# Linear-attention constants in a pool of their own made one stage earlier, and a fifth pair of the down projection by seven products

## The chip, the cores and the metric

One Trainium2 chip, of which the program uses one core. The metric is the device time of one execution in microseconds (us). The engines are TensorE (PE in the profile; its weight loads are PEld), VectorE (DVE), ScalarE (ACT), GpSimd (POOL) and SyncE (SP, which here issues transfers only).

## The reference

A trunk of four layers on a float32 input of 256 rows and 1024 columns. Each layer is a token mixer and a feed-forward part, and both end in a residual and a layer norm:

```python
for i in range(DEPTH):                      # DEPTH = 4
    kind = i % 3                            # 0 band attention, 1 gated linear attention, 2 differential attention
    y = mixer[kind](h)
    h = layer_norm(DN_ALPHA * h + y, ln1_g[i], ln1_b[i])
    g, u = split(h @ w_gate_up[i])          # 1024 -> 2 * 2816
    h = layer_norm(DN_ALPHA * h + (silu(g) * u) @ w_down[i], ln2_g[i], ln2_b[i])
```

The gated linear attention (the second layer's mixer) computes, beside its queries, keys, values and output gate, `log_a = log_sigmoid((x @ w_g1) @ w_g2 + b_g) / 16`, cumulative sums of it in chunks of 64 rows, a state for each chunk, and an rms norm with a gain `g_norm`.

## The kernel before

**Arithmetic.** Each float32 product is made of three TensorE products of rounded operands: every operand is split into a high part and a rest (`wh`, `wl` of the weights; two halves of `xT`, `plain`, `seven` of the data), and high by high, rest by high and high by rest are summed in PSUM. For every weight tile that arrives, ScalarE therefore casts the high part (L132, L145) and VectorE subtracts it for the rest (L133, L146) before TensorE can use it.

**Buffers.** Raw weights land in a ring of 24 KB per partition, split weights lie in a ring of 64 KB, in the order in which they are asked for; a split tile waits until the products that read the older tile at its place are done. Longer-lived tiles lie in the pool `act` (the residual `h`, the transposed input `xT`, small statistics with 16 buffers of each tag, `k1`). Everything else lies in a pool of the stage (`in_stage`: one mixer or one feed-forward part), opened when the stage begins and closed at its end; the next stage's pool takes the same place, and a tile there waits for the older tiles that it overlaps.

**Order.** The program is written out in full, without loops on the chip. `run_rows` and `run_cols` go through the weight tiles of a product; a clock of steps (`tick`) starts deferred pieces (`defer`): transposes of a finished norm, gate products, splits. A scheduler turns this into a fixed order of instructions for each engine, in which work that is ready may go ahead of earlier work that is not; on the chip each engine keeps that order.

**The mixer of layer 2** (`gla`, L656). It begins with its constants: a tile `cst` with a triangle of ones, the gain `g_norm` and two indicator columns; `g1t` with the split `w_g1` (memset L686, cast L687, subtraction L688); and `g2` with `w_g2` twice and `b_g` (memset L695, transfers L696 to L698). Then `gate1` (L716) is deferred by 2 steps, `gate2` (L736) by 3 more, `gate3` (L749) by 8 more, among the products of keys and output gate.

**The feed-forward part** (`ffn`). The 2816 hidden columns are 11 pairs of 128-column blocks. The up projection makes the pairs in order. A pair that is in `SEVEN = (0, 2, 4, 6)` is kept as four 128x128 blocks for each block product; GpSimd makes four sums and differences of them (`combine`), and ScalarE and VectorE split the seven results (`split`). The others are put into `plain`. The down projection goes through the pairs 0 to 7, loading pair c+1 before the products of pair c, and then the tail, pairs 8 to 10, first all rows of the first half (`t` = 0), then of the second:

- an ordinary pair takes 8 products of three matmuls each (`step`), and two casts and two subtractions of 128x1024 elements for its weights;
- a pair in `SEVEN` takes 7 products of three matmuls (`seven_products`), and for its weights three sums and differences on VectorE (L1017: one of 128x1024, two of 128x512 elements) and the casts and subtractions of seven blocks (one of 128x512, two of 128x1536 elements).

With the last pair of `SEVEN`, `gather` adds the sums that only these pairs use to `h`: nine VectorE additions of 128x512 elements, each after a product of that pair.

```python
for c in range(n_pairs - 3):
    load(c + 1)
    if c in SEVEN:
        seven_products(c)
        continue
    ...
for c in tail[1:]:
    load(c)
```

Of the kernel before, what the change touches and what calls it, by code (L numbers as in the profile page):

```python
# [9 lines left out]
F32 = mybir.dt.float32  # L10
F32R = mybir.dt.float32r
# [4 lines left out]
P = 128  # L16
# [17 lines left out]

SEVEN = (0, 2, 4, 6)


@with_exitstack  # L40
def trunk_kernel(
# [33 lines left out]
    act = ctx.enter_context(tc.tile_pool(name="act", bufs=1))  # L75
# [4 lines left out]
    def nm(s):  # L80
        uid[0] += 1
        return f"{s}_{uid[0]}"
# [5 lines left out]
    def in_stage(fn, *args, **kw):  # L88
        with tc.tile_pool(name=nm("stage"), bufs=1, reuse_waits="tile") as pool:
            stage.append(pool)  # L90
            fn(*args, **kw)
            stage.pop()

    def st(shape, dtype, tag, bufs):
        return stage[-1].tile(shape, dtype, tag=tag, bufs=bufs, name=nm(tag))

    def slab(shape, dtype=F32):
        return st(shape, dtype, "slab", 3)
# [4 lines left out]
    def k2(shape, dtype=F32):  # L103
        return st(shape, dtype, "k2", 12)
# [1 line left out]
    def k1(shape, dtype=F32):  # L106
        return act.tile(shape, dtype, tag="k1", bufs=5, name=nm("k1"))

    def small(shape, tag="small", bufs=16):
        return act.tile(shape, F32, tag=tag, bufs=bufs, name=nm(tag))  # L110

    def bank(tag="tp"):
# [5 lines left out]
    pad = const.tile([P, 32], F32, tag="powt", name="powt")  # L118
# [154 lines left out]
    def input_operand():  # L273

        return act.tile([P, NKT, 4 * P], F32R, tag="xT", bufs=1, name=nm("xT"))
# [377 lines left out]
        out_proj(OT, w_o, norm)  # L653


    def gla(xT, norm):  # L656
        HK, HV, NH = 128, 256, 4
        w_in = b_w_in
        w_g1, w_g2, b_g, g_norm = b_w_g1[0], b_w_g2[0], b_b_g[0], b_g_norm[0]
        cst = k2([P, 512])  # L660
        upper, gn, ind = cst[:, 0:P], cst[:, P : P + HV], cst[:, P + HV : P + HV + 2]
        nc.gpsimd.memset(cst, 0.0)
        for a in range(2):
# [17 lines left out]

        g1 = k1([P, NKT, 16])
        nc.gpsimd.dma_start(g1, w_g1.rearrange("(k p) n -> p k n", p=P))
        g1t = k2([P, 512], F32R)
        g1s = g1t[:, : 48 * NKT].rearrange("p (k n) -> p k n", n=48)
        nc.gpsimd.memset(g1t.bitcast(F32), 0.0)  # L686
        nc.scalar.copy(out=g1s[:, :, 0:16], in_=g1)  # L687
# [3 lines left out]
            in1=g1s[:, :, 0:16].bitcast(F32),  # L691
            op=ALU.subtract,
        )
        g2 = k2([P, 512])
        nc.gpsimd.memset(g2, 0.0)  # L695
        nc.gpsimd.dma_start(g2[0:16, :], w_g2)  # L696
        nc.gpsimd.dma_start(g2[32:48, :], w_g2)
        nc.gpsimd.dma_start(g2[64:65, :], b_g.unsqueeze(0))  # L698

        vo = slab([P, 2, 2, D])  # L700
        v, O = vo[:, 0, :, :], vo[:, 1, :, :]
# [190 lines left out]
    def ffn(xT, layer, norm):  # L892
# [8 lines left out]
        n_pairs = FFN // 256  # L901
        rest = [c for c in range(n_pairs) if c not in SEVEN]
        plain = st([P, 2 * len(rest), 4 * P], F32R, "plain", 1)

        def place_of(c):
            return 2 * rest.index(c)
# [17 lines left out]
        def split(c, f):  # L924
            x = seven[c] = st([P, 2, 7, P], F32R, "seven", len(SEVEN))
            nc.scalar.copy(out=x[:, 0], in_=f[:, 0:7, :])
            nc.vector.tensor_tensor(
                out=x[:, 1], in0=f[:, 0:7, :], in1=x[:, 0].bitcast(F32), op=ALU.subtract
            )
# [11 lines left out]
        def turn_hidden(c, t, hd):  # L941
            b = bank()
            for k in range(2):
                ks = slice(k * P, (k + 1) * P)
                nc.tensor.transpose(b[:, ks], hd[:, ks], ident)
            if c not in SEVEN:
                put(
# [17 lines left out]
        def col_done(c):  # L965
            g = {}

            def done(blk, b):
# [8 lines left out]
                gg = g.pop(k)  # L977
                if c not in SEVEN:
                    nc.vector.tensor_tensor(out=lo, in0=lo, in1=gg, op=ALU.mult)
# [15 lines left out]
        for c in range(2, FFN // 256):  # L995
            run_cols(w[c], src, col_done(c))
            if c >= 7:
                k = place_of(c)
                norm.load(
                    plain[:, k, 0:1].bitcast(F32), lambda sh: st(sh, F32, "gb", 4)  # L1000
                )
# [4 lines left out]
        def load(c):  # L1006
            raw = raw_ring.tile([P, 4, 512], F32, name=nm("raw"))
            nc.sync.dma_start(raw, w_down[layer, c].rearrange("p (k n) -> p k n", k=4))
            if c not in SEVEN:
                parts[c] = halves(raw[:, 0:2], 2) + halves(raw[:, 2:4], 2)  # L1010
# [39 lines left out]
        def seven_products(c):  # L1050
            for i, (a, b) in FORMS.items():
# [4 lines left out]
                    parts[c][b],  # L1056
                    c == SEVEN[-1] and i not in where,
                )
# [63 lines left out]
    xT = input_operand()  # L1122
# [11 lines left out]
    for i in range(depth):  # L1134
        kind, j = i % 3, i // 3
        norm1 = Norm(h, ln1_g[i], ln1_b[i])
        if i == 0:
            norm1.loads = [
                (h[t], None, x[0, t * P : (t + 1) * P, :]) for t in range(2)
            ] + norm1.loads  # L1140
            first = dict(src=first_src, lag=2, fine=4, warm=WARM)
        else:
            first = {}
        if kind == 0:
            in_stage(
                attention, xT, a_w_qkv[j], a_bias[j], a_w_o[j], norm1, False, **first
            )
        elif kind == 1:
            in_stage(gla, xT, norm1)
        else:  # L1150
            in_stage(attention, xT, c_w_qkv, c_bias, c_w_o, norm1, True)
        norm2 = Norm(h, ln2_g[i], ln2_b[i], out[0] if i == depth - 1 else None)
        in_stage(ffn, norm1.xT, i, norm2)
        xT = norm2.xT

    act.tile([P, 8], F32, tag="pad", bufs=1, name="pad")


def _layouts(inputs):
# [82 lines left out]
```

## Time and profile before

| | us |
|---|---|
| median of three runs | 1213.64 (1213.18 to 1213.73) |
| the profiled execution's own time | 1212.91 |
| its span, first to last instruction | 1211.2 |
| TensorE busy | 1193.0 |
| VectorE busy | 913.0 |
| ScalarE busy | 682.7 |
| GpSimd busy | 153.7 |

The own time of the profiled execution is 1.7 us over its span, and 0.7 us under the median of the runs. TensorE's matmuls overlap, so their listed durations are longer than the time from one to the next; the starts are what counts. The mean granted TensorE clock was 0.994 of full speed.

### The profile page before, as it was taken

The page shows a single profiled execution, that of the slowest core. Times are in us where ns is not written, and L with a number is a line of the kernel's source. Part 1 is how long each engine was busy: PE and PEld are TensorE (multiplying, and loading weights), DVE is VectorE, ACT ScalarE, POOL GpSimd, SP SyncE. Part 2 cuts the span into 40 slices and gives each one's busy share as a digit, 9 for nine tenths or more (in the row PEclk, how much of TensorE's full clock was granted, in tenths as well). Part 3 has the DMA queues.
Part 4 walks back from the last instruction along what each step waited for, and adds up shares of the span by engine and source line. Part 5 has one row for each costly group of instructions (what it writes and reads, how often), then busy time and mean ns, then how long its engine had stood idle before and what let it go on. Part 6 is the DMA issues. An engine that isn't in the chain of part 4 may idle for free.

```text
span 1211.2 us, 17131 instructions
## 1 busy us (share of the span) xinstructions
PE 1193.0 (98%) x6200; PEld 989.5 (82%) x6200; DVE 913.0 (75%) x1502; ACT 682.7 (56%) x1185; POOL 153.7 (13%) x284
## 2 busy tenths in 40 slices
PE   9999999999999999999999999999999999999996
PEld 7888888888677888888887778888888888888885
DVE  6688776887556777778867786678886888676985
ACT  6566565664474446656446656556535774665650
POOL 1220112000210011110022210110002200101000
PEclk9999999999899999999999999999999999999998
DMA  9653645555464465556564355564557544655450
GB/s 366 216 183 122 226 152 197 198 191 187 147 230 135 139 208 191 175 189 219 206 220 156 124 162 187 198 198 163 229 176 250 192 134 153 202 172 201 161 204 35
DMA packets 56692, 223.87 MB, mean 185 GB/s; under 512 B 6816, under 2 KB 7328, under 8 KB 50976
## 3 DMA queue, kind: packets, MB, share of 16 engines
q1 hardware_dynamic: 51264, 206.59, 50.0%
q0 software_dynamic: 4768, 15.15, 4.0%
q8 instruction: 48, 0.79, 0.3%
q10 hardware_dynamic: 576, 1.05, 0.3%
q14 instruction: 36, 0.29, 0.1%
HBM read 221.71 MB, written 1.05 MB: 184 GB/s over the span
## 4 chain that ended last, share of the span: by engine, by line
PE 89%; DVE 4%; DMA 2%; ACT 2%; POOL 2%; issue 1%; POOLq 0%; DVEq 0%; ACTq 0%
PE mm L231 26%; PE mm L232 13%; PE mm L210 8%; PE mm L211 8%; PE mm L212 8%; PE tp L1029 5%; PE tp L1030 5%; PE tp L1031 5%; PE tp L470 2%; PE mm L1029 1%; PE mm L1031 1%; PE mm L1030 1%; PE tp L259 1%; DVE wl L133 1%; PE tp L539 1%
## 5 line engine op out<-in xcount | busy, mean ns | idle before, releaser
L231 PE MATMUL mm<-xT,wh 128*128 128x512 f32 x1568 | 555.0, 397 | 0.0
L232 PE MATMUL mm<-xT,wl 128*128 128x256 f32 x1568 | 440.6, 281 | 0.0
L133 DVE TENSOR_TENSOR wl<-raw,wh 128x1024 fp32r<-128x1024 f32 (+1 forms) x306 | 368.1, 1211 | 61.8 <-ACT wh L132 58.6
L132 ACT CAST wh<-raw 128x1024 fp32r<-128x1024 f32 (+1 forms) x306 | 314.4, 1045 | 111.6 <-PE mm L211 59.7
L231 PEld LDWEIGHTS mm<-xT,wh 128*128 128x128 f32 x1568 | 294.2, 188 | 70.0 <-issue 4.6
L232 PEld LDWEIGHTS mm<-xT,wl 128*128 128x128 f32 x1568 | 296.5, 189 | 0.7 <-issue 0.3
L210 PE MATMUL mm<-wh,xT 128*128 128x512 f32 x304 | 121.2, 402 | 0.9 <-ACT wh L132 0.9
L212 PE MATMUL mm<-wl,xT 128*128 128x512 f32 x304 | 119.2, 394 | 0.9 <-DVE wl L133 0.9
L211 PE MATMUL mm<-wh,xT 128*128 128x512 f32 x304 | 119.6, 395 | 0.0
L146 DVE TENSOR_TENSOR wl<-raw,wh 128x1024 fp32r<-128x1024 f32 (+2 forms) x88 | 104.4, 1218 | 12.7 <-ACT wh L145 9.0
L145 ACT CAST wh<-raw 128x1024 fp32r<-128x1024 f32 (+2 forms) x88 | 90.3, 1050 | 24.0 <-PE tp L1031 13.1
L1029 PE MATMUL tp<-wl,plain 128*128 128x512 f32 x224 | 88.9, 397 | 0.0
L1030 PE MATMUL tp<-wh,plain 128*128 128x512 f32 x224 | 88.4, 395 | 0.0
L1031 PE MATMUL tp<-wh,plain 128*128 128x512 f32 x224 | 88.4, 395 | 0.0
L971 DVE TENSOR_TENSOR k<-mm,k 128x256 f32<-128x256 f32 x144 | 60.3, 419 | 36.6 <-ACT k L970 36.5
L970 ACT COPY k<-mm 128x256 f32<-128x256 f32 x144 | 53.0, 368 | 44.0 <-PE mm L232 43.8
L210 PEld LDWEIGHTS mm<-wh,xT 128*128 128x128 f32 x304 | 57.3, 189 | 15.7 <-issue 1.8
L212 PEld LDWEIGHTS mm<-wl,xT 128*128 128x128 f32 x304 | 57.4, 189 | 14.2 <-DVE wl L133 2.8
L211 PEld LDWEIGHTS mm<-wh,xT 128*128 128x128 f32 x304 | 57.4, 189 | 13.3 <-issue 1.2
L284 POOL TENSOR_SCALAR sm<-mv 128x1 f32<-128x1 f32 x16 | 11.9, 746 | 372.0 <-DVE mv L348 372.0
L210 PE MATMUL mm<-wh,slab 128*128 128x512 f32 x128 | 51.5, 404 | 0.0
L211 PE MATMUL mm<-wh,slab 128*128 128x512 f32 x128 | 51.1, 399 | 0.0
(190 smaller groups left out, 1535.9 us busy)
## 6 DMA issues: line engine op xcount, KB each, us to landing
raw<-in_w_gu_dram SPq DMA_DIRECT2D x176, 512.0 KB, 4.3
raw<-in_w_down_dram SPq DMA_DIRECT2D x44, 1024.0 KB, 4.9
raw<-in_a_qkv_dram SPq DMA_DIRECT2D x46, 512.0 KB, 4.8
raw<-in_b_in_dram SPq DMA_DIRECT2D x24, 512.0 KB, 4.3
raw<-in_c_qkv_dram SPq DMA_DIRECT2D x24, 512.0 KB, 4.4
raw<-in_a_o_dram SPq DMA_DIRECT2D x16, 512.0 KB, 3.9
k<-in_a_bias_dram POOLq DMA_DIRECT2D x16, 256.0 KB, 4.7
raw<-in_b_o_dram SPq DMA_DIRECT2D x8, 512.0 KB, 3.8
```

The source lines that it names most:

```text
L132: nc.scalar.copy(out=wh[:, k, :], in_=raw[:, k, :])
L133: nc.vector.tensor_tensor(out=wl[:, k, :], in0=raw[:, k, :], in1=wh[:, k, :].bitcast(F32), op=ALU.subtract,)
L145: nc.scalar.copy(out=wh, in_=w)
L146: nc.vector.tensor_tensor(out=wl, in0=w, in1=wh.bitcast(F32), op=ALU.subtract)
L210: nc.tensor.matmul(b, xh, wh, start=first, stop=False)
L211: nc.tensor.matmul(b, xl, wh, start=False, stop=False)
L212: nc.tensor.matmul(b, xh, wl, start=False, stop=last)
L231: nc.tensor.matmul(b, wh[:, cs], xk, start=kt == 0, stop=False)
L232: nc.tensor.matmul(b[:, :256], wl[:, cs], xk[:, :256], start=False, stop=kt == NKT - 1)
L1029: nc.tensor.matmul(o, xh, wl, start=start, stop=False)
L1030: nc.tensor.matmul(o, xh, wh, start=False, stop=False)
L1031: nc.tensor.matmul(o, xl, wh, start=False, stop=stop)
```

## The change

The constants of the linear attention are made by a new function, `gla_consts`, which is called when the feed-forward part of the layer before begins, after that layer's mixer has ended; they lie in a pool of their own (`gc`, three buffers of 2 KB) that stays open until the mixer that uses them has ended. Pair 7 joins `SEVEN`, so that its products are seven, and the pair's weights, blocks and gathering follow the form of the others; the transfer of a gain for the norm that was tied to pair 7's block is tied to the nearest ordinary pair before it, pair 5. To make room, the small tiles get 12 buffers instead of 16; a padding tile grows from 8 to 40 elements.

```diff
-SEVEN = (0, 2, 4, 6)
+SEVEN = (0, 2, 4, 6, 7)
...
-    def small(shape, tag="small", bufs=16):
+    def small(shape, tag="small", bufs=12):
...
-    def gla(xT, norm):
-        HK, HV, NH = 128, 256, 4
-        w_in = b_w_in
+    def gla_consts(pool):
+        HV = 256
         w_g1, w_g2, b_g, g_norm = b_w_g1[0], b_w_g2[0], b_b_g[0], b_g_norm[0]
-        cst = k2([P, 512])
+        cst = pool.tile([P, 512], F32, tag="gc", bufs=3, name=nm("gc"))
...
-        g1t = k2([P, 512], F32R)
+        g1t = pool.tile([P, 512], F32R, tag="gc", bufs=3, name=nm("gc"))
...
-        g2 = k2([P, 512])
+        g2 = pool.tile([P, 512], F32, tag="gc", bufs=3, name=nm("gc"))
...
+        return upper, gn, ind, g1t, g2
+
+    def gla(xT, norm, consts):
+        HK, HV, NH = 128, 256, 4
+        w_in = b_w_in
+        upper, gn, ind, g1t, g2 = consts
...
             if c >= 7:
-                k = place_of(c)
+                k = place_of(max(r for r in rest if r <= c))
...
         elif kind == 1:
-            in_stage(gla, xT, norm1)
+            in_stage(gla, xT, norm1, consts)
+            gc.close()
...
+        if i + 1 < depth and (i + 1) % 3 == 1:
+
+            gc = ExitStack()
+            consts = gla_consts(
+                gc.enter_context(tc.tile_pool(name=nm("gc"), bufs=1, reuse_waits="tile"))
+            )
         in_stage(ffn, norm1.xT, i, norm2)
...
-    act.tile([P, 8], F32, tag="pad", bufs=1, name="pad")
+    act.tile([P, 40], F32, tag="pad", bufs=1, name="pad")
```

## Rows read from the trace of the kernel before

**Rows 1.** The page, busy us, share of the span, instructions.

```profile
PE 1193.0 (98%) x6200; PEld 989.5 (82%) x6200; DVE 913.0 (75%) x1502; ACT 682.7 (56%) x1185; POOL 153.7 (13%) x284
```

**Rows 2.** TensorE's waits over the whole span, by the releaser.

```profile
engine line waited for: us in total, times, longest us
PE tp L736 <- DMA k<-in_b_b_g_dram: 2.5, 1, 2.5
```

**Rows 3.** Timeline of TensorE around its longest wait (start, duration, idle before).

```profile
316.98 0.39 PE L212 MATMUL mm<-wl,xT 128*128 128x512 f32 x1
319.90 1.19 PE L736 MATMUL tp<-k,k 65*128 65x512 f32 x1 [2.54 <-DMA k<-in_b_b_g_dram]
```

**Rows 4.** Stretches: length, busy time of each engine, PEclk, DMA share, GB/s.

```profile
core 0: us, PE busy (x) PEld busy (x) DVE busy (x) ACT busy (x) POOL busy (x), PEclk, DMA share, GB/s
319.90:326.20 6.30, 6.29 (x16) 4.34 (x17) 1.02 (x2) 3.91 (x6) 0.00 (x0) 0.50 0.00 0
844.70:849.30 4.60, 4.05 (x18) 2.97 (x17) 4.60 (x7) 4.57 (x6) 0.00 (x0) 1.00 0.61 233
```

**Rows 5.** Timeline of GpSimd where layer 2's mixer begins.

```profile
310.12 0.94 POOL L288 TENSOR_TENSOR sm<-sm,powt 128x1 f32<-128x1 f32 x1
311.01 0.53 POOL L662 MEMSET k<- 128x512 f32 x1
...
317.05 0.48 POOL L698 DMA_DIRECT2D k<-in_b_b_g_dram  x1
```

**Rows 6.** Timeline of GpSimd from 101 to 142 us, its last instruction there.

```profile
126.78 0.94 POOL L288 TENSOR_TENSOR sm<-sm,powt 128x1 f32<-128x1 f32 x1
```

**Rows 7.** Timeline of TensorE in layer 1's down projection.

```profile
277.28 0.39 PE L1029 MATMUL mm<-wl,seven 128*128 128x512 f32 x1
277.51 0.39 PE L1030 MATMUL mm<-wh,seven 128*128 128x512 f32 x1
...
290.52 0.39 PE L1029 MATMUL tp<-wl,plain 128*128 128x512 f32 x1
```

**Rows 8.** Timeline of VectorE there, 253 to 274 us.

```profile
254.53 1.21 DVE L1017 TENSOR_TENSOR tt<-raw 128x1024 f32<-128x1024 f32 x1
...
258.09 1.76 DVE L146 TENSOR_TENSOR wl<-tt,wh 128x1536 fp32r<-128x1536 f32 x1 [0.90 <-ACT wh L145]
259.88 1.23 DVE L1017 TENSOR_TENSOR tt<-raw 128x1024 f32<-128x1024 f32 x1
261.03 4.02 DVE L146 TENSOR_TENSOR wl<-raw,wh 128x1536 fp32r<-128x1536 f32 x3
...
269.55 4.07 DVE L146 TENSOR_TENSOR wl<-raw,wh 128x1536 fp32r<-128x1536 f32 x3
```

**Rows 9.** Timeline of VectorE there, 273 to 290 us.

```profile
276.48 1.23 DVE L146 TENSOR_TENSOR wl<-raw,wh 128x1024 fp32r<-128x1024 f32 x1 [2.86 <-ACT wh L145]
...
285.30 3.48 DVE L146 TENSOR_TENSOR wl<-raw,wh 128x1024 fp32r<-128x1024 f32 x3
```

**Rows 10.** Timelines of VectorE in the down projections of layers 2 and 4.

```profile
569.28 2.89 DVE L146 TENSOR_TENSOR wl<-raw,wh 128x1536 fp32r<-128x1536 f32 x2
...
584.42 3.48 DVE L146 TENSOR_TENSOR wl<-raw,wh 128x1024 fp32r<-128x1024 f32 x3
...
1166.63 2.89 DVE L146 TENSOR_TENSOR wl<-raw,wh 128x1536 fp32r<-128x1536 f32 x2
...
1182.02 3.48 DVE L146 TENSOR_TENSOR wl<-raw,wh 128x1024 fp32r<-128x1024 f32 x3
```

**Rows 11.** Timelines of TensorE there, the first matmul on pair 10's second weight tile.

```profile
590.29 0.40 PE L1029 MATMUL tp<-wl,plain 128*128 128x512 f32 x1
...
1187.95 0.39 PE L1029 MATMUL tp<-wl,plain 128*128 128x512 f32 x1
```

**Rows 12.** Stretch of layer 1's down projection up to pair 10's first product.

```profile
276.50:289.80 13.30, 13.30 (x59) 10.78 (x58) 13.30 (x16) 7.65 (x8) 0.00 (x0) 1.00 0.52 174
```

**Rows 13.** Groups by line over the span: count, busy us, mean ns, idle before.

```profile
L146 DVE TENSOR_TENSOR wl<-raw,wh 128x1536 fp32r<-128x1536 f32 x16 | 28.0, 1750 | 0.0
L247 DVE TENSOR_TENSOR plain<-k,plain 128x256 fp32r<-128x256 f32 x48 | 20.2, 421 | 9.9 <-ACT plain L246 9.9
L927 DVE TENSOR_TENSOR seven<-hid,seven 128x896 fp32r<-128x896 f32 x16 | 17.5, 1092 | 34.9 <-ACT seven L926 34.9
```

**Rows 14.** Transfer issues over the span: count, KB each, us to landing.

```profile
raw<-in_w_down_dram SPq DMA_DIRECT2D x44, 1024.0 KB, 4.9
```

## Prediction

> **What bounds the kernel now.** I read the page first: TensorE is busy for 1193.0 of 1211.2 us, and VectorE, the next, for 913.0 [rows 1]. Time can come only from fewer matmuls, from TensorE's few waits, or from a stretch at a lower clock; and it is lost wherever another engine falls behind. TensorE's waits come next: the longest by far is 2.5 us, once, at L736, the second gate product of the linear attention, for the bias `b_g` [rows 2]. The timeline shows that place: L212 starts at 316.98 and L736 at 319.90 [rows 3]. The view of stretches shows what follows: from 319.90 to 326.20 the granted clock is 0.50, the lower of the two levels (1.2 instead of 2.4 GHz), although TensorE works all that time [rows 4]. What it had done before was to stand idle for 2.5 us. After a gap of 0.9 us in layer 3's down projection the clock stays at 1.00 [rows 4].
>
> Last, the down projections on VectorE. In layer 1, from 276.50 to 289.80, VectorE is busy for all 13.30 us [rows 12]: it splits the last three pairs' weights and gathers, just ahead of the matmuls that read them. TensorE waits for nothing there, but the margin is small; it is worked out below.
>
> **The constants.** In the kernel before, their memsets follow the norm's last GpSimd step at 310.12, and the last transfer, `b_g`, is issued at 317.05 [rows 5], while the mixer's program asks for `gate1` after two steps and for `gate2` three steps later. Made one stage earlier, they are there some 180 us before they are needed. What goes away:
> - the wait: from 316.98 to 319.90 is 2.92 us, of which one matmul's normal spacing is 0.23 (277.28 to 277.51 [rows 7]): 2.69 us;
> - the low clock: 6.30 us at 0.50 does the work of 3.15: another 3.15 us.
>
> Sum 5.84 us. Bounds: with the gates earlier, `gate2` may come to wait for VectorE, which serves the norm just then; half of the wait, 1.3 us, could come back, so 4.5; above, 6.5, if the smaller waits in that stage go too.
>
> Where they go, layer 1's feed-forward part, GpSimd has no more work after 126.78 until past 142 [rows 6], so the memsets, the selection and five transfers (311.01 to 317.53, 6.5 us [rows 5]) pass through its queue in front of nothing urgent: cost nothing. Behind the cast of `g1` on ScalarE stand the casts of `xT` for the second rows; if that cast has to wait for its transfer they are late and TensorE stops as it did before. I take nothing (the `g1` tile is in `act`, free long before); the upper bound is the same 5.84 us moved.
>
> **Pair 7, TensorE.** 21 instead of 24 matmuls, four times: 12 x 0.23 = 2.8 us saved.
>
> **Pair 7, up projection.** VectorE's two puts (2 x 0.42) become one split of 1.09 us, plus four GpSimd additions [rows 13]: 0.25 us more VectorE per layer, three column groups before anyone reads it. Hidden by those groups; without them 4 x 0.25 = 1 us. The gain's transfer goes by pair 5 and is issued earlier; the buffers from 16 to 12 free slots long unused: nothing.
>
> **Pair 7, its weights.** This is the dear part. Now pair 7 takes VectorE two subtractions of 1024. After, it takes what pair 4 took: from the first difference at 254.53 to the end of its last subtraction (the first of the three from 261.03, which lasts 1.75 [rows 13]) at 262.78, 8.25 us; less 1.15 for pair 6's difference in between (259.88 to 261.03) and plus about 0.6 for the subtraction of 512: 7.7 us, of which 0.90 is a wait for ScalarE's cast that nothing filled [rows 8]. It can begin when pair 6's last subtraction ends, 269.55 + 1.75 = 271.30, since both use the one `tt` buffer. Pair 7 is then done at 279.0, against 273.62 now. The idle 2.86 us that VectorE has before 276.48 is eaten [rows 9].
>
> After it VectorE has the same 15 instructions as now: six subtractions for pairs 8 to 10 and nine additions of `gather`, from 276.48 to 285.30 + 3.48 = 288.78, 12.3 us without a gap [rows 9]. They now end at 279.0 + 12.3 = 291.3. `gather` moves from pair 6 to pair 7, but stands before the loads of pairs 9 and 10 in the program, so pair 10 stays last. TensorE wants pair 10's second tile at 290.52 now [rows 7], and 0.7 earlier after, at 289.82. It stops for 291.3 - 289.8 = 1.5 us. The same sum for layer 2: 569.28 + 1.75 + 20.0 = 591.0 against 590.29 - 0.70, 1.4 us; for layer 4, 1166.63 + 1.75 + 20.0 = 1188.4 against 1187.25, 1.1 us [rows 10, 11]; layer 3 I take like layer 1. Together 5.5 us, in each layer twice what the three matmuls give.
>
> Bounds: if the scheduler lets pair 10's tiles pass the last three additions, or fills the cast's 0.90 us and the short gaps between dependent differences, 1.4 us comes off each stop, and nearly nothing is left: 0. Above: pair 10's transfer starts only when pair 7's raw tile is free, about 279.0, and lands 4.9 us later [rows 14], at 283.9, still ahead of its turn; with a slow one or one more unfilled wait I allow 2.2 us a layer, 8.8. Behind it in SyncE's queue stand the next stage's first weights, which TensorE reads only after the tail: nothing. I take 5.5, the sum as the rows give it.
>
> One rule of the Trainium skill speaks against this. "VectorE: DVE Perf Modes", section "The TRN2 errata", gives a float32 tensor_tensor a time of (N+151)/0.96 ns with a fixed part for every instruction; by it (an estimate) six of 1024 and nine of 512 elements take 13.6 us, not 12.3, and the four stops would be 5 us longer. The trace agrees on a single one (1.23 us) and not on a row of them. The rival below is worked from rows alone.
>
> **Sum.** The profiled execution's own time of 1212.91, less 5.84, less 2.8, plus 5.5: 1209.8. The median of the runs is 0.73 higher, so the forecast for it is 1213.64 - 3.1 = 1210.5 us, 0.26% less. A difference of 0.2% (2.4 us) is about what a measurement of this kernel can tell from none.
>
> **Rivals.**
> - *No stop in the tail* (pair 10's tiles go ahead of the additions, or the gaps are filled). For it: the scheduler fills gaps where it can, and only 1.4 us a layer is needed. Against: it left 0.90 us unfilled for pair 4 [rows 8]. Stops of 0 to 2 us in all: 1213.6 - 8.6 = 1205.0 to 1207.0.
> - *Longer stops, no gain in all.* ScalarE's casts or pair 10's transfer come late too; 2.2 us a layer: 1213.6 - 8.6 + 8.8 = 1213.8.
> - *Slower: the stops lower the clock.* The 2.5 us wait did, the 0.9 us gap did not [rows 4]; 1.5 us lies between. Each such layer costs 3.15 us more: from two layers on the gain is gone (1210.5 + 6.3 = 1216.8), with four it is 1223.1.
> - *The wait is only moved*: `g1`'s cast holds ScalarE where layer 1's feed-forward part begins: 1210.5 + 5.8 = 1216.3. Against it: the transfer of `g1` needs no place in a stage pool.
> - *Every VectorE instruction at full length.* Three subtractions in a row took 3.48 where one alone took 1.23 [rows 9], so a join saves 0.10; without the 14 joins each stop is 1.4 us longer: 1210.5 + 5.6 = 1216.1. The rows that it would have to change are those it contradicts.
>
> **How the numbers follow.** Forecast 0.50 (its own range 1208.5 to 1212.5, a third of it within 2.4 us of no change), no stop 0.23, longer stops 0.13, lower clock 0.08, moved wait 0.03, full length 0.03. Faster: 0.33 + 0.23 = 0.56; same: 0.17 + 0.13 = 0.30; slower: 0.14. The range goes down to the whole of the no-stop case, 1205.0, and up past the longer stops, 1214.0; the last three lie outside.
>
> **What would show it.** Right: no wait at L736 and a clock of 1.00 all through layer 2's mixer; VectorE without idle time from pair 6 to pair 10; TensorE waiting for L146 on pairs 9 and 10 in each down projection, 1 to 1.5 us, at full clock. Wrong: no such waits (the first rival), waits over 2 us or a clock of 0.50 after them (the second and third), or a wait in the first 15 us of layer 1's feed-forward part (the fourth). The forecast falls most easily with the order that the scheduler gives the nine additions and the last four subtractions.

## Result and the profile after

The changed kernel takes 1200.12 us (median of 4 runs, 1198.73 to 1202.67) beside 1213.41 (1212.80 to 1213.73) for the kernel before on the same chip: ratio 0.9897, 95% interval 0.988 to 0.9913. In a second group of runs it took 1200.39 (ratio 0.99, 0.9886 to 0.9913). The forecast was 1210.5 with a range down to 1205.0; the time lies 5 us below the range. The sign was right and the size was not: 13.3 us came off, not 3.1.

The page of the profiled execution of the changed kernel (own time 1199.89); columns as in [rows 1]:

```profile
PE 1183.2 (99%) x6188; PEld 984.3 (82%) x6188; DVE 929.8 (78%) x1514; ACT 687.6 (57%) x1185; POOL 165.6 (14%) x300
...
PEclk9999999999999999999999999999999999999999
```

TensorE has 12 instructions fewer and 9.8 us less busy time; VectorE has 16.8 us more, and hardly any of it shows in TensorE's waits (below). 12 matmuls are 2.8 us, so 7 us of TensorE's own time went some other way; half of the slow stretch of [rows 4], 3.15 us, is busy time too, and that leaves some 4 us that no term of the forecast held. (Busy time is the time that the listed matmuls cover, so matmuls that stand closer make it smaller.)

TensorE's waits after (what waited, for whom, us in total, times, longest):

```profile
PE mm L202 <- POOL ident masks.py:199: 1.4, 1, 1.4
PE mm L210 <- ACT wh L132: 1.0, 2, 0.9
PE tp L259 <- DVE h L367: 0.8, 2, 0.6
PE mm L212 <- DVE wl L133: 0.5, 1, 0.5
PE tp L581 <- DVE k L513: 0.3, 1, 0.3
PE mm L211 <- DVE xT L247: 0.3, 1, 0.3
PE tp L626 <- DVE k L613: 0.2, 1, 0.2
```

Two things are to be seen by their absence. L736 [rows 2] is gone, as forecast. And L146, the weights of the down projection, for which four waits of 1.1 to 1.5 us were forecast, is not there at all.

The place of the old wait, in stretches, first of the kernel after, then of the kernel before on either side of what [rows 4] show (us, PE busy, weight load, DVE, ACT, POOL, clock, DMA):

```profile
303.00:312.00 9.00, 9.00 (x46) 7.24 (x45) 8.24 (x14) 4.67 (x7) 2.94 (x2) 1.00 0.52 171
312.00:320.00 8.00, 7.75 (x40) 5.75 (x39) 5.04 (x8) 5.80 (x8) 0.00 (x0) 1.00 0.57 197
320.00:334.00 14.00, 14.00 (x66) 11.10 (x66) 7.41 (x8) 11.65 (x15) 0.00 (x0) 1.00 0.42 135
```

```profile
304.00:317.00 13.00, 12.62 (x60) 10.11 (x58) 11.33 (x18) 2.67 (x4) 7.54 (x13) 1.00 0.72 234
...
326.20:342.00 15.80, 15.28 (x73) 11.52 (x72) 9.89 (x11) 14.74 (x19) 0.00 (x0) 1.00 0.49 164
```

The clock is at 1.00, the upper level, throughout. TensorE's idle time beside the long wait was 0.38 + 0.52 = 0.90 us and is 0.25 now. From the stage's first row product (L210, at 304.64 before and 303.32 after) to its first column product (L231, at 342.16 and 333.99) the traces have 37.52 us before and 30.67 after: 6.85 less.

The matmuls themselves stand closer. TensorE in layer 1's down projection after, a stretch as long as that of [rows 7]:

```profile
277.30 0.39 PE L1035 MATMUL mm<-wh,seven 128*128 128x512 f32 x1
...
289.99 0.39 PE L1034 MATMUL tp<-wl,plain 128*128 128x512 f32 x1
```

Both stretches, 277.30 to 289.99 here and 277.51 to 290.52 in [rows 7], span 56 matmuls without a wait. Before it is 13.01 us, 232.3 ns each; after, 12.69 us, 226.6 ns each. Nothing is idle and the clock is the same; the spacing changed. Over all four down projections, steps over 260 ns left out, it was 232.3 to 233.3 ns and is 226.8 to 227.3; in the output products that take their stationary operand from a stage pool (L210 to L212 on a `slab`) it was 232.2 to 232.6 and is 227.4 to 228.6; in the row products with `xT` it is 227 to 229 in both kernels.

Why no stop came shows on VectorE. Layer 1 after, the stretch that answers to [rows 9]:

```profile
276.47 2.88 DVE L146 TENSOR_TENSOR wl<-raw,wh 128x1536 fp32r<-128x1536 f32 x2
280.22 2.36 DVE L146 TENSOR_TENSOR wl<-raw,wh 128x1024 fp32r<-128x1024 f32 x2 [0.86 <-ACT wh L145]
282.49 0.68 DVE L325 SCALAR_TENSOR_TENSOR h<-h,mm 128x512 f32<-128x512 f32 x1
283.09 1.22 DVE L146 TENSOR_TENSOR wl<-raw,wh 128x1024 fp32r<-128x1024 f32 x1
285.39 1.22 DVE L146 TENSOR_TENSOR wl<-raw,wh 128x1024 fp32r<-128x1024 f32 x1 [1.08 <-ACT wh L145]
286.53 0.68 DVE L1078 TENSOR_TENSOR tt<-mm,tt 128x512 f32<-128x512 f32 x1
287.13 1.21 DVE L146 TENSOR_TENSOR wl<-raw,wh 128x1024 fp32r<-128x1024 f32 x1
288.26 1.28 DVE L325 SCALAR_TENSOR_TENSOR h<-h,tt 128x512 f32<-128x512 f32 x2
289.47 1.28 DVE L322 TENSOR_TENSOR h<-mm,h 128x512 f32<-128x512 f32 x2
290.67 0.68 DVE L325 SCALAR_TENSOR_TENSOR h<-h,tt 128x512 f32<-128x512 f32 x1
291.26 1.28 DVE L322 TENSOR_TENSOR h<-mm,h 128x512 f32<-128x512 f32 x2
```

The first row holds the last of pair 7 (to 278.22) and the first of pair 8. Pair 10's last subtraction is the one from 287.13, done at 288.34; two of the nine additions of `gather` (282.49 and 286.53) stand ahead of it, the other seven, from 288.26, behind it. In the kernel before all nine stood ahead of it, the last two of them here, in front of the three subtractions from 285.30 of [rows 9]:

```profile
284.10 1.28 DVE L322 TENSOR_TENSOR h<-mm,h 128x512 f32<-128x512 f32 x2
```

Layer 4 after has the order of layer 1. Layer 2 after is otherwise:

```profile
573.60 0.68 DVE L325 SCALAR_TENSOR_TENSOR h<-h,mm 128x512 f32<-128x512 f32 x1
574.20 1.22 DVE L146 TENSOR_TENSOR wl<-raw,wh 128x1024 fp32r<-128x1024 f32 x1
575.34 0.68 DVE L1078 TENSOR_TENSOR tt<-mm,tt 128x512 f32<-128x512 f32 x1
576.05 1.29 DVE L325 SCALAR_TENSOR_TENSOR h<-h,tt 128x512 f32<-128x512 f32 x2
577.26 1.28 DVE L322 TENSOR_TENSOR h<-mm,h 128x512 f32<-128x512 f32 x2
578.46 0.68 DVE L325 SCALAR_TENSOR_TENSOR h<-h,tt 128x512 f32<-128x512 f32 x1
579.06 1.28 DVE L322 TENSOR_TENSOR h<-mm,h 128x512 f32<-128x512 f32 x2
580.26 2.35 DVE L146 TENSOR_TENSOR wl<-raw,wh 128x1024 fp32r<-128x1024 f32 x2
```

Here all nine additions come first and pair 10 is done at 582.61, as the forecast's sum has it. But TensorE's order is another. TensorE there:

```profile
581.21 0.39 PE L1035 MATMUL tp<-wh,plain 128*128 128x512 f32 x1
581.53 0.50 PE L1034 MATMUL tp<-wl,plain 128*128 128x512 f32 x1
```

The round of three products is broken off: after L1035 (581.21) no L1036 follows but the next tile's L1034, pair 10's first, as soon as its subtraction has ended (581.47). Pair 10's two tiles are first read by the 198th and 203rd of the stage's 249 matmuls in layers 2 and 3, and by the 190th and 193rd, as written, in layers 1 and 4. The step to 581.53 is 0.32 us and the next one 0.34, where 0.227 is the rule: TensorE stops for 0.20 us there and for 0.25 us in the same place in layer 3, too short for the view of waits to list. How long a tile of pair 10 was ready before it was read (tiles A and B, from the traces):

| | layer 1 | layer 2 | layer 3 | layer 4 |
|---|---|---|---|---|
| before | 2.19, 1.74 | 2.83, 2.38 | 2.16, 1.71 | 2.88, 2.45 |
| after | 1.34, 0.29 | 0.05, 0.19 | 0.05, 0.19 | 2.18, 1.13 |

### The profile page after: what moved, and what is told of

Same layout as the page of the kernel before. It is cut to its first block, busy times and chain, and to the rows that moved or that the text cites. A ratio compares the mean times of both kernels' runs of the same rounds, so it can differ in the third digit from the quotient of the medians.

```text
span 1198.2 us, 17122 instructions
## 1 busy us (share of the span) xinstructions
PE 1183.2 (99%) x6188; PEld 984.3 (82%) x6188; DVE 929.8 (78%) x1514; ACT 687.6 (57%) x1185; POOL 165.6 (14%) x300
## 4 chain that ended last, share of the span: by engine, by line
PE 63%; DVE 7%; ACT 2%; issue 1%; POOL 1%; DMA 0%; POOLq 0%; DVEq 0%; ACTq 0%
PE mm L231 21%; PE mm L232 11%; PE mm L210 6%; PE mm L211 6%; PE mm L212 6%; PE tp L1034 2%; PE tp L1036 2%; PE tp L1035 2%; DVE wl L146 2%; DVE wl L133 1%; PE tp L470 1%; PE tp L259 1%; ACT k L493 1%; PE mm L1036 1%; PE mm L1035 1%
## 5 line engine op out<-in xcount | busy, mean ns | idle before, releaser
L231 PE MATMUL mm<-xT,wh 128*128 128x512 f32 x1568 | 556.4, 398 | 0.0
L133 DVE TENSOR_TENSOR wl<-raw,wh 128x1024 fp32r<-128x1024 f32 (+1 forms) x306 | 368.0, 1211 | 64.3 <-ACT wh L132 60.8
L231 PEld LDWEIGHTS mm<-xT,wh 128*128 128x128 f32 x1568 | 294.4, 188 | 71.1 <-issue 4.6
L210 PE MATMUL mm<-wh,xT 128*128 128x512 f32 x304 | 121.2, 401 | 1.1 <-ACT wh L132 1.0
L212 PE MATMUL mm<-wl,xT 128*128 128x512 f32 x304 | 118.6, 392 | 0.5 <-DVE wl L133 0.5
L146 DVE TENSOR_TENSOR wl<-raw,wh 128x1024 fp32r<-128x1024 f32 (+1 forms) x88 | 103.6, 1218 | 4.6 <-ACT wh L145 4.5
L1034 PE MATMUL tp<-wl,plain 128*128 128x512 f32 x192 | 75.2, 393 | 0.0
L1035 PE MATMUL tp<-wh,plain 128*128 128x512 f32 x192 | 74.8, 389 | 0.0
L1036 PE MATMUL tp<-wh,plain 128*128 128x512 f32 x192 | 74.5, 390 | 0.0
L210 PEld LDWEIGHTS mm<-wh,xT 128*128 128x128 f32 x304 | 57.0, 188 | 15.8 <-issue 2.0
L212 PEld LDWEIGHTS mm<-wl,xT 128*128 128x128 f32 x304 | 57.1, 188 | 13.3 <-DVE wl L133 1.8
L284 POOL TENSOR_SCALAR sm<-mv 128x1 f32<-128x1 f32 x16 | 15.2, 950 | 363.2 <-DVE mv L348 363.2
L145 ACT CAST wh<-tt 128x1536 fp32r<-128x1536 f32 x20 | 29.6, 1480 | 45.9 <-DVE tt L1022 42.1
L932 DVE TENSOR_TENSOR seven<-hid,seven 128x896 fp32r<-128x896 f32 x20 | 21.8, 1092 | 43.1 <-ACT seven L931 43.1
```

The source lines that it names most:

```text
L133: nc.vector.tensor_tensor(out=wl[:, k, :], in0=raw[:, k, :], in1=wh[:, k, :].bitcast(F32), op=ALU.subtract,)
L145: nc.scalar.copy(out=wh, in_=w)
L146: nc.vector.tensor_tensor(out=wl, in0=w, in1=wh.bitcast(F32), op=ALU.subtract)
L210: nc.tensor.matmul(b, xh, wh, start=first, stop=False)
L212: nc.tensor.matmul(b, xh, wl, start=False, stop=last)
L231: nc.tensor.matmul(b, wh[:, cs], xk, start=kt == 0, stop=False)
```

## Experiments

After the first comparison there were two theories for the 10 us that the forecast missed. *A:* the smaller `small` buffers and the other `pad` move every stage pool 128 bytes down in each partition (139136 to 139008), and the place of the stationary operand sets the matmuls' spacing; the stops were taken away by the order. *Rival:* the spacing comes with the change itself (fewer plain pairs, other traffic), and the pools' place does nothing. The addresses are those that the program gives its tiles; no trace holds them, and the shifts between the runs follow from the edits. The first four runs share their runs of the kernel before: 1212.46 (1209.35 to 1214.80).

**The pools alone.**

```diff
-    def small(shape, tag="small", bufs=16):
+    def small(shape, tag="small", bufs=12):
...
-    act.tile([P, 8], F32, tag="pad", bufs=1, name="pad")
+    act.tile([P, 40], F32, tag="pad", bufs=1, name="pad")
```

> The kernel before with the small tiles' 12 buffers and the padding tile of 40 elements alone, so that every stage pool lies 128 bytes lower, as in the changed kernel. Theory A (the place of the stage pools sets how fast TensorE takes a stationary operand from them: 0.227 instead of 0.232 us from matmul to matmul in the down projections and in the mixers' output products): about 996 + 384 matmuls by 5 ns, 6 to 7.5 us faster, 1206 to 1207.5 us, with 0.227 us in the trace. Rival B (the shorter spacing comes with pair 7's form or with the order): no change, 1213.4 us, spacing 0.232.

Measured: 1207.81 (1206.15 to 1209.67), ratio 0.9962 (0.9949 to 0.9976): 4.65 us less, 2.9 to 6.2. The spacing is 227 ns in all four down projections and 227 to 229 in the `slab` products. The gain is below the 6 to 7.5 us that was expected, but clear of none. An edit that the forecast costed at nothing, and that leaves every engine the same instructions in the same order, is worth more than the forecast for the whole change.

**Pair 7 alone**, at the old place of the pools.

```diff
-SEVEN = (0, 2, 4, 6)
+SEVEN = (0, 2, 4, 6, 7)
...
-                k = place_of(c)
+                k = place_of(max(r for r in rest if r <= c))
```

> The kernel before with pair 7 in SEVEN (and the gain tied to pair 5) alone. Theory A (the order of TensorE was made anew, so no stop in the tail, and only the 12 matmuls count): 2.8 us faster, 1210.6 us, no waits of TensorE for L146 over 0.5 us, spacing 0.232. Rival C (as predicted): stops of 1.1 to 1.5 us in each down projection, 1216 us. Rival B: spacing 0.227 and 9 us faster.

Measured: 1210.2 (1208.13 to 1212.09), ratio 0.9982 (0.9971 to 0.9993): 2.3 us less, 0.8 to 3.5, where 12 matmuls are 2.8. There is no wait for L146, and the spacing is 232 to 233 ns, so neither the pair nor its order makes the matmuls closer. L736's wait is there and is 2.9 us long. This run is also the nearest to the forecast's own setting. In its layer 2 pair 10's last subtraction (the second of those from 588.48) is done at 590.83, and the matmul that would have been the first to read it in the order as written, the 193rd, starts at 589.28, 1.5 us too early:

```profile
588.48 2.35 DVE L146 TENSOR_TENSOR wl<-raw,wh 128x1024 fp32r<-128x1024 f32 x2
```

```profile
589.28 0.39 PE L1029 MATMUL tp<-wl,plain 128*128 128x512 f32 x1
...
590.45 0.40 PE L1029 MATMUL tp<-wl,plain 128*128 128x512 f32 x1
```

The forecast's sum for this layer was 1.4 us. But here too pair 10 is first read by the 198th matmul (590.45) and the 203rd, and no step there is longer than 0.24 us.

**The constants alone**, at the old place: the parts of the diff that concern `gla_consts`, its pool and its call.

```diff
+        if i + 1 < depth and (i + 1) % 3 == 1:
+
+            gc = ExitStack()
+            consts = gla_consts(
+                gc.enter_context(tc.tile_pool(name=nm("gc"), bufs=1, reuse_waits="tile"))
+            )
```

> The kernel before with the constants in their own pool one stage earlier alone; pools stay at the old residue. Theory A and the prediction's term alike: the wait of 2.69 us and 3.15 us at half clock go, 5.8 us faster, 1207.6 us. If the mixer loses less than that now or the wait is moved: under 4 us.

Measured: 1204.87 (1204.21 to 1206.96), ratio 0.994 (0.9927 to 0.9952): 7.6 us less, 5.8 to 8.9. No wait at L736.

**The whole change with the pools at their old place.**

```diff
-    act.tile([P, 40], F32, tag="pad", bufs=1, name="pad")
+    act.tile([P, 72], F32, tag="pad", bufs=1, name="pad")
```

> The changed kernel with 32 elements more in the padding tile, so that the stage pools lie where they lay before (128 bytes higher than in the change). Theory A: 6 to 7.5 us slower than the changed kernel, about 1206 to 1207.5 us, spacing 0.232 in the down projections. Rival B: no difference, 1200 us.

Measured: 1203.56 (1202.85 to 1205.14), ratio 0.9928 (0.9916 to 0.9941): 8.9 us less, with 232 to 233 ns in the down projections. That is 3.4 us more than the changed kernel's 1200.12, half of the 6 to 7.5 expected. So without the pools' place the change gives some 9 us; the place gives the rest. The three parts alone sum to 4.65 + 2.3 + 7.6 = 14.5; the whole gave 12.1 to 13.3 in its two groups of runs.

**What about the place matters?** The place moved relative to two things: to multiples of 256 (139136 is 128 past one, 139008 is one), and to the weights' ring, from which the moving operand comes. Four runs tell these apart; in the first and the third everything is shifted by 128 with a larger tile at the front of the partition.

```diff
-    pad = const.tile([P, 32], F32, tag="powt", name="powt")
+    pad = const.tile([P, 64], F32, tag="powt", name="powt")
```

> The kernel before with 128 bytes more at the front of each partition, so that the weights' ring, xT and the stage pools all begin 128 bytes later: the stage pools at 139264, a multiple of 256; xT (115584) and the ring (41856) at 128 past one. Theory A, the address of the stationary operand itself decides (multiple of 256 bytes or not): down projections and output products with a stationary operand from the stage pool fall from 232 to 227 ns from start to start, row products with xT rise from 227 to 232; the gain of some 5 us of the run with the lower pools is given back on xT's roughly 900 matmuls (4 to 5 us): time 1210 to 1214. If the column products, whose stationary weights lie in the ring, rise too, 5 us more. Theory B, stationary and moving operand must lie alike: xT products stay at 227, down projections stay at 232, time as before, 1212.5.

```diff
-    def small(shape, tag="small", bufs=16):
+    def small(shape, tag="small", bufs=12):
...
-    act.tile([P, 8], F32, tag="pad", bufs=1, name="pad")
+    act.tile([P, 56], F32, tag="pad", bufs=1, name="pad")
```

> The kernel before with the stage pools only 64 bytes lower (139072, 64 past a multiple of 256; the run of 128 lower was at 0 past one, the kernel before is at 128). Theory A, a step at multiples of 256: 232 ns in the down projections, time as before (1212.5). Variant, any multiple of 64 but not 128 past: 227 ns, 1208. Variant, a cost that grows with the offset: 229 to 230 ns, 1210.

The third has the edits of the run of the pools alone and the larger tile of the first of these four:

```diff
-    def small(shape, tag="small", bufs=16):
+    def small(shape, tag="small", bufs=12):
...
-    pad = const.tile([P, 32], F32, tag="powt", name="powt")
+    pad = const.tile([P, 64], F32, tag="powt", name="powt")
...
-    act.tile([P, 8], F32, tag="pad", bufs=1, name="pad")
+    act.tile([P, 40], F32, tag="pad", bufs=1, name="pad")
```

> The kernel before with the weights' ring and xT 128 bytes higher and the buffers at 12, so that the stage pools lie at 139136 again, where they lie in the kernel before, and 97,280 bytes above the ring, as in the run with the pools 128 lower. Theory A, the stationary operand's own address decides: 232 ns in the down projections, 1212. Theory B, what counts is how the stationary operand lies to the moving one in the ring: 227 ns at the very address that took 232, and 1207 to 1209.

The fourth moves only the pools, up:

```diff
-    act.tile([P, 8], F32, tag="pad", bufs=1, name="pad")
+    act.tile([P, 40], F32, tag="pad", bufs=1, name="pad")
```

> The kernel before with the stage pools 128 bytes higher (139264, which is 97,536 above the ring: a multiple of 256 and not of 512). At this address of the pools 232.4 was measured with the ring 128 higher. Theory B with multiples of 256: 227 ns and 1207 to 1209. Theory B with multiples of 512 or more: 232 ns and 1212 to 1213. Theory A with another multiple: as the run at the same pool address, 232 ns.

Measured, with what went before; the spacing is the mean from start to start over layer 4's down projection (in the run 64 lower without a wait of 0.2 us for another tile), the distance is that of the pools' first byte from the ring's:

| run | pools at | ring at | distance, past a multiple of 256 | ns | us |
|---|---|---|---|---|---|
| before | 139136 | 41728 | 128 | 233.3 | 1212.46 |
| pools 128 lower | 139008 | 41728 | 0 | 227.0 | 1207.81 |
| pools 64 lower | 139072 | 41728 | 64 | 233.3 | 1213.63 |
| pools 128 higher | 139264 | 41728 | 0 | 226.9 | 1207.19 |
| everything 128 higher | 139264 | 41856 | 128 | 233.3 | 1215.11 |
| the same pools, ring 128 higher | 139136 | 41856 | 0 | 226.8 | 1210.93 |

All six have the same instructions in the same order on every engine. The kernel before took 1212.46 beside the run 128 lower, 1211.78 beside those of 64 lower and of everything higher, and 1212.53 beside the other two. With everything 128 higher the first three layers have 232.4 ns.

TensorE, the first and the last of layer 4's 252 matmuls, first with everything 128 higher, then with the pools where they are before and the ring higher:

```profile
1142.44 0.39 PE L1029 MATMUL mm<-wl,seven 128*128 128x512 f32 x1
...
1201.01 0.40 PE L1031 MATMUL tp<-wh,plain 128*128 128x512 f32 x1
```

```profile
1143.73 0.40 PE L1029 MATMUL mm<-wl,seven 128*128 128x512 f32 x1
...
1200.65 0.39 PE L1031 MATMUL tp<-wh,plain 128*128 128x512 f32 x1
```

58.57 us against 56.92 for the same 251 steps. My first theory, that the stationary operand's own address decides, falls twice: 139136 takes 233.3 ns with the ring at 41728 and 226.8 with the ring at 41856, and 139264 the other way round. What decides is the distance of the pools from the ring, and so of the stationary operand from the moving one: a multiple of 256 bytes is quick, 64 or 128 past one is slow. (What moved with the ring, the raw weights, `h` and `xT`, the runs don't part from it.) `xT` lies 73,728 bytes above the ring (288 times 256) in every run, and its products are at 227 to 229 ns in every one.

The splits that ScalarE and VectorE write into the ring are not needed for it. In layer 4 before, the last of them is done at 1185.50, and the last matmul starts at 1201.02; in between ScalarE does nothing and VectorE works on the norm alone:

```profile
1186.00:1201.00 15.00, 15.00 (x66) 12.05 (x65) 6.77 (x12) 0.00 (x0) 1.10 (x2) 1.00 0.10 35
```

Those 66 steps still take 233.3 ns each, and in the kernel after the 60 steps behind its last split take 226.7.

Three ratios are not explained by these spacings alone. The run 64 lower is 1.9 us slower than before (1.0018, 1.0009 to 1.0027); it has 233.3 ns in all four down projections, where the kernel before has 232.3 to 232.4 in three, and 233.2 to 233.3 in the `slab` products against 232.2 to 232.6, some 1.2 us in all. Everything 128 higher is 3.3 us slower (1.0022, 1.001 to 1.0034), and the run with the same pools and the ring higher gains 1.6 us (ratio 0.9984, 0.9975 to 0.9992) where the two others at 227 ns gain 4.7 and 5.3. Some 3 us a run are lost elsewhere when the ring and `xT` move up by 128. The profiled run of the latter has all four up projections at their slower spacing (below); whether that is the rule there stays open.

**More work on VectorE in the tail.**

```diff
             elif i == 6:
+                for _ in range(3):
+                    nc.vector.tensor_tensor(
+                        out=u[0], in0=u[0], in1=norm.h[0][:, 0:512], op=ALU.add
+                    )
                 nc.vector.tensor_tensor(out=u[0], in0=bk[6], in1=u[0], op=ALU.add)
```

> The changed kernel with three additions of 512 more on VectorE behind pair 7's second product, in each layer (1.8 us a layer at 0.60 each; the sum of the hidden states is altered by them). Theory A, the order of the instructions takes it up (pair 10's two subtractions go ahead of seven or eight of the additions, and TensorE reads them on time): no wait of TensorE for L146, at most the norm behind the tail is later by 0 to 1.8 us a layer where VectorE ends the stage; 1200 to 1204. Theory B, as in the prediction's sum (VectorE's work in the tail is on the path): the additions come in front of pair 10 and TensorE waits 1.8 us longer less the slack of 0.05 to 1.1 us seen after: 5.5 to 7 us more, 1206 to 1208.

Measured: 1202.2 (1201.4 to 1203.51), ratio 0.9919 (0.9906 to 0.9933), about 2 us more than the changed kernel and not 5.5 to 7. The order changed again: in all four layers pair 10's last subtraction now has no more than four of twelve additions ahead of it, TensorE keeps its written order, and the tiles are ready 0.60 us or more before they are read. There is no wait for L146. The first theory holds for this much work: it goes behind pair 10.

**Pair 10 wanted later.**

```diff
-        for n in range(2):
-            for c in tail:
+        for c in tail:
+            for n in range(2):
                 for k in range(2):
                     step(0, n, c, k, (c, k) == end)
```

> The changed kernel with the first rows' tail taken pair by pair (both column halves of pair 8, then 9, then 10), so that pair 10 is wanted 12 matmuls, 2.7 us, later than as written. Theory A, there is no stop left in the tail: the same time, 1199 to 1202 (a little later if the first half's norm, which now ends 12 matmuls later, holds VectorE up at the end). Theory B, some of the computed stops are there but hidden from the view of waits (up to 0.3 us a layer): 0.5 to 1.2 us less.

Measured: 1200.72 (1200.1 to 1202.85), ratio 0.9908 (0.9894 to 0.9922): the time of the changed kernel. The margin of pair 10's second tile grows to 3.99, 0.43, 0.38 and 3.83 us, and the short stops of layers 2 and 3 are gone from the trace. They are 0.45 us in all, at the lower end of what the second theory asks for; the runs, 2.8 us apart, cannot show so little. The trace settles it: there was a stop, and it was 0.45 us and not 5.5.

**A sixth pair by seven products.** With the tail by pairs, in layers 2 to 4; in layer 1 the constants' pool takes the room.

```diff
-SEVEN = (0, 2, 4, 6, 7)
+FIVE = (0, 2, 4, 6, 7)
+SIX = (0, 2, 4, 5, 6, 7)
...
         n_pairs = FFN // 256
+        SEVEN = FIVE if layer == 0 else SIX
```

> The tail by pairs, and in layers 2 to 4 pair 5 by seven products too (layer 1 has no room beside the constants). TensorE does 9 matmuls less: 2.0 us at 0.227. VectorE does some 3.6 us more in each of the three down projections, where it stood idle 2.6 to 5.2 us of 46 to 48. Theory A, order and idle time take it up again: 1197.5 to 1199.5. Theory B, VectorE is now the bound of that stage: 2 to 3.5 us of waits for L147 in each of three layers, 1204 to 1209.

Measured: 1209.77 (1208.34 to 1211.63), 9.4 us more than the changed kernel beside it. TensorE's longest waits:

```profile
PE tp L260 <- DVE h L368: 5.2, 2, 2.6
PE mm L1036 <- DVE wl L147: 2.1, 3, 0.7
```

Here VectorE does become the bound, and most of the price is not where the second theory put it: 2.1 us for the weights, but 5.2 in two waits for the norm behind the tail (L260 is L259 of the changed kernel), which has been pushed back. So the order moves the debt to the next stage's start; with five pairs the same wait is 0.8 us. Behind the first of the two waits at L260 the granted clock stays at its upper level, behind the second it falls (last section).

**The changed kernel again**, with the last runs.

> The changed kernel again, beside the others on the same chip: 1198.7 to 1202.7, as in its first four runs, with 227 ns in the down projections.

Measured: 1200.39 (1197.96 to 1201.52), with 227 ns. No kernel tried is faster.

## Why the prediction was wrong

Three steps carry the 10.4 us between 1210.5 and 1200.1: 5.05 of the forecast's 5.5 us of stops did not come, the pools' place gave 4.65 and the constants 1.0 more; that is 10.7, and 0.5 goes off for pair 7, which gave 2.3 and not 2.8. The runs of one kernel lie 2 to 4 us apart, so the sum is no closer than that.

**The step that failed first: "They now end at 279.0 + 12.3 = 291.3", and TensorE "stops for 291.3 - 289.8 = 1.5 us"; in four layers +5.5.** It measured 0.45, and nothing in the run of pair 7 alone. The cost of pair 7 on VectorE was about right: forecast done at 279.0, measured 278.22. The order was not. In layers 1 and 4 seven of the nine additions pass behind pair 10, and in layer 1 VectorE is done with it at 288.34, 3.0 earlier than forecast, although it waited 1.94 us for ScalarE. In layers 2 and 3 VectorE does what the forecast says: in layer 2 the stage begins 8.24 us earlier than before, and 582.61 + 8.24 = 590.9 against 591.0. There I held TensorE's order fixed as in [rows 11], and that order gave way: in the run of pair 7 alone the lateness against the written order is 1.5 us where 1.4 was computed, and no stop comes of it, because eight matmuls of other tiles go ahead. In the changed kernel TensorE, with its closer steps, is there earlier; as written, the tile would have been wanted at 578.95 + 6 x 0.227 = 580.31, a stop of 2.3 us, and it is read at 582.80 behind one of 0.20. Both orders are fixed when the kernel is built, and both were rebuilt with the change. The bound named for this case (0, if pair 10 passes the additions) was the right end. The prediction held the scheduler able to do it and gave "no stop" 0.23.

**The step that was missing: "the buffers from 16 to 12 free slots long unused: nothing".** It is worth 4.65 us by itself (2.9 to 6.2), and 5.3 with the pools moved the other way (1207.19 against 1212.53; 3.3 to 6.5 by its interval). By the rows, 996 matmuls of the down projections and 384 of the output products at some 5 ns come to 6.9 us, a little above what the runs give. The prediction begins with a list of where time can come from: fewer matmuls, waits, the clock. The step from one matmul to the next is not on it. No row of before shows this as a wait; what it shows is 0.23 us for the spacing in [rows 7], and I used it as one number for all matmuls. Set beside each other, the stages of the kernel before differ: 227 ns with `xT` and 232 with a pool's operand. That difference was there to be asked about.

**The constants: right in kind, 1 us small.** Forecast 5.84, with 6.5 as the upper bound; 6.85 by the stage, 7.6 (5.8 to 8.9) by the runs. In the execution that the rows come from, the wait (2.69) and the slow clock (3.15) are as computed; 0.65 us more are the stage's smaller waits (0.90 to 0.25), which I had put at the bound. That the clock's part came out is in part luck: in three of the seven traces that have this wait the low stretch is half as long (last section).

**The rival of a lower clock** rested on one stop that lowered it and one that did not. The second was put at 0.9 us; that is its step from start to start, and its idle time is 0.55 ([rows 4]: 4.05 of 4.60 us busy), while the 2.5 us of the first is idle time. No stop of 1.5 us came in the changed kernel's down projections, so what four of them would have done to the clock stays open. The last section has stops of 1.4 to 2.6 us elsewhere: length alone does not decide.

**Right:** the cast of `g1` held nothing up; the matmuls saved (2.3 measured, 0.8 to 3.5; 2.8 forecast); the clock at its upper level all through layer 2; VectorE's joined rows as in [rows 9] (2.35 for two). The case without stops was put at 1205.0 to 1207.0; with the pools at their old place, the only setting that it describes, the change ran in 1203.56, which the constants' missing 1.0 to 1.8 us accounts for. The 1200.12 of the change itself is that case and the pools' place together, which no rival held.

## What to carry to other kernels

A stop computed for an order of instructions holds only while that order is kept; ask first who makes the order, and if it is made anew with each build, put a case in which independent work fills a computed lateness of 1 or 2 us, on the late engine or on the waiting one, ahead of the stop. Here that held with five pairs and with three additions more, and no longer with a sixth pair, whose work was more than the stage could hold. Compare the start-to-start spacing of the same instruction across stages before any change: a few ns that differ between operands of different pools were worth more here than any one wait, with over a thousand such matmuls. And an edit that only changes the size of a buffer moves everything allocated above it; it is a change to be costed and run by itself.

## What the hardware showed that was not expected

*The distance between the two operands of a matmul.* 128x512 products follow each other at 227 ns when the stationary operand lies a multiple of 256 bytes per partition from the moving one, and at 232 to 233 when it lies 64 or 128 past one. TensorE shows no wait. The Trainium skill, "TensorE: Matmul & The Clock Gate", section "Step-by-step: what each phase is for", gives TensorE two independent read ports and says that loading the next weights takes no read bandwidth from the running matmul. The section gives no reason why the place should matter; in these runs it costs 5 to 6 ns a matmul, and the measurement decides. The difference is there with no split being written into the ring, which points to TensorE's own reads of the two operands. That is argued, not shown, and no run here shows why 256 is the step.

*The price of a stop is not fixed.* The granted clock (the third number from the end) behind four of TensorE's stops: two of 2.62 us at L260 in the run with a sixth pair; one of 1.46 us at L626 in the run with three additions more, one of 1.41 us at L626 in the run of the pools alone.

```profile
596.40:602.50 6.10, 5.69 (x26) 4.17 (x27) 6.10 (x10) 1.17 (x2) 1.14 (x2) 1.00 0.25 63
899.00:902.20 3.20, 3.20 (x9) 2.02 (x8) 3.20 (x6) 0.71 (x2) 0.00 (x0) 0.50 0.00 0
```

```profile
645.90:649.20 3.30, 3.30 (x15) 2.12 (x14) 1.22 (x7) 0.31 (x1) 2.10 (x6) 0.50 0.30 76
```

```profile
651.00:658.00 7.00, 7.00 (x44) 5.56 (x44) 3.90 (x18) 3.68 (x15) 2.74 (x9) 1.00 0.35 95
```

Of two stops alike one lowered the clock and one did not, at 2.6 us and at 1.4. And behind the wait at L736, of 2.5 to 3.3 us in seven traces (the kernel before, pair 7 alone and the five runs that move only buffers), the clock was low every time, but for 6.8 us in four of them and 3.4 in three: 3.4 or 1.7 us lost. One execution gives one such price.

*Two speeds of the same stage.* An up projection's 288 pairs of column products take one of two lengths in every trace kept here, 100.05 us or 101.7 to 101.8. In the execution after, layers 1 and 3, first and last of 288 matmuls of L231:

```profile
144.68 0.40 PE L231 MATMUL mm<-xT,wh 128*128 128x512 f32 x1
...
244.72 0.39 PE L231 MATMUL mm<-xT,wh 128*128 128x512 f32 x1
...
732.12 0.39 PE L231 MATMUL mm<-xT,wh 128*128 128x512 f32 x1
...
833.88 0.40 PE L231 MATMUL mm<-xT,wh 128*128 128x512 f32 x1
```

100.04 against 101.76 us, with no wait listed in either and a clock of 1.00; the next matmul follows L231's after 230 or 236 ns. Before, the stages of layers 1 to 4 were quick, quick, quick, slow; after, quick, quick, slow, slow; with the constants alone, all quick. One stage is 1.7 us, so a good part of the 2 to 4 us between runs of one kernel can come from this; what sets it is open.
